# One decoder step in fp32: where the last operand pieces of a gate/up pair stand among the products of the next pair

## The chip, the cores and the metric

The kernel runs on one core of a Trainium2 chip. The metric is device time in microseconds (us) of one execution; lower is better. Engines are named as in the profile: PE (TensorE), DVE (VectorE), ACT (ScalarE), POOL (GpSimd), and SP, whose queue issues the transfers.

## What is computed

One inference step of a two-layer decoder trunk over 1024 prompt tokens and 8 sample tokens, so T = 1032 columns. Each of the two layers ends in a SwiGLU block, and that block is what the change is about:

```python
D_MODEL = 1024
D_FF = -(-8 * D_MODEL // (3 * 256)) * 256   # 2816
...
def swiglu(h, w_gu, w_down):
    g, u = jnp.split(h @ w_gu, 2, axis=-1)
    return (jax.nn.silu(g) * u) @ w_down
...
    for l in range(N_A_LAYERS):
        out, st = short_conv(rmsnorm(x, norm_a[l]), conv_prefix[l], w_in_a[l], conv_w[l], w_out_a[l])
        x = x + out
        x = x + swiglu(rmsnorm(x, norm_ffn[l]), w_gu[l], w_down[l])
...
        x = x + o @ w_o[l]
        li = N_A_LAYERS + l
        x = x + swiglu(rmsnorm(x, norm_ffn[li]), w_gu[li], w_down[li])
```

## The kernel before

Activations lie with features on the 128 partitions and tokens along the free axis. Every fp32 product is made of three matmuls: an operand is split into a high part (ACT copies it to the matmul type) and a low part (DVE subtracts the high part from the operand), and high·high, high·low and low·high are added in PSUM. `split` (lines 147 to 150) does this for weights and activations; `put` (lines 511 to 530) does it for hidden pieces.

The gate and up projections and part of the down projection use a Strassen-like scheme with seven products in place of eight. `gate_up` (line 469) makes 22 units per layer: unit 2m is the gate and unit 2m+1 the up projection of pair m. A unit has the seven products in the order `SEVEN = (1, 5, 6, 3, 7, 2, 4)`. A product is 24 matmuls of 258 columns (two column halves, four blocks of the contraction, three matmuls each). Products 1, 6, 7 and 4 add up in one PSUM tile X, 5 and 3 in Y, 2 in Z. Since product 6 goes on adding to what product 1 left, X must be copied out between them, and so must Y between products 5 and 3:

```python
            if p == 1:
                S.activation(p1[:, s], X, AF.Copy)
            elif p == 5:
                S.activation(p5[:, s], Y, AF.Copy)
```

These are lines 551 to 554 in `gate_step`; they are called **the copy of product 1** (L552) and **the copy of product 5** (L554) below. Product 6 of the gate unit waits for the first and product 3 for the second.

After products 3, 7, 2 and 4 of the up unit the four quarters of silu(gate)·up are complete (`up_step`, lines 570 to 594; the last of them is the multiply of line 593). For pairs 0 to 7 `finish` (line 532) turns them into the seven operands of the seven-product down projection, called pieces 1 to 7: some are quarters, some are differences of quarters. For each piece `put` makes a high part (ACT, L521) and a low part (DVE, L522) in one of four columns of `x` that are used in turn (`ring`, line 478), and SP writes it to DRAM (L524). Pieces 7 and 3 come after product 7; piece 1, a subtraction (L540), piece 5, a subtraction (L542) and piece 6 after product 2; piece 2, a subtraction (L546) and piece 4 after product 4. A slot of the ring is free again when its write has landed: of a pair's seven pieces, piece 6 takes the slot of piece 7, piece 2 that of piece 3, piece 4 that of piece 1.

Weights: `pair_units` (line 416) fetches a unit's weights on SP, POOL forms the four sums that the scheme needs (L446, L448, L450, L452), and ACT and DVE split all seven weight blocks (L149, L150).

The program is recorded in the order of the text, and a scheduler then decides each engine's order. Each engine runs its own list strictly in that order. So the place of an instruction in the text does not say where it stands on its engine.

The words **boundary** and **tail** are used below for the passage from the up unit of pair m to the gate unit of pair m+1, for m from 0 to 7 in each layer (16 in all), and for the pieces that are made there.

Of the kernel before, what the change touches and what calls it, by code (L numbers as in the profile page):

```python
# [13 lines left out]
ALU = mybir.AluOpType  # L14
# [42 lines left out]
def trunk_kernel(ctx, tc, A):  # L57
    nc = tc.nc
    V, S, G, PE, Q = nc.vector, nc.scalar, nc.gpsimd, nc.tensor, nc.sync
# [401 lines left out]
    def col(t, i):  # L461
        return t[:, i * TH : (i + 1) * TH].rearrange("p (s c) -> p s c", s=2)
# [3 lines left out]
    def three_banks():  # L466
        return [pools[-1][0].tile([P, 2, 512], F32, name="mm2") for _ in range(3)]

    def gate_up(layer, us):
# [3 lines left out]
        sg = {  # L473
            q: col(x[:, (3, 7)[i // 2]], i % 2) for i, q in enumerate((11, 12, 21, 22))
        }
# [23 lines left out]
        def group(ps, w, p, s, first):  # L499
            wh, wl = w[p]  # L500
            for k in range(4):
                xh, xl = operand(p, k, s)
                c = slice(k * P, (k + 1) * P)
                for i, (lhs, rhs) in enumerate(((wh, xh), (wh, xl), (wl, xh))):
                    PE.matmul(  # L505
                        ps[:, s, :TS], lhs[:, c], rhs, start=first and k == 0 and i == 0,
                        stop=k == 3 and i == 2, skip_group_check=not first,
                    )
            tick()

        def put(m, src, q=None, p=None):


            nonlocal puts
            k = ring[puts % 4]
            puts += 1
            hi, lo = col(x[:, k], 0), col(x[:, k], 1)
            if src is None:
                G.tensor_tensor(lo, sg[22], sg[12], op=ALU.subtract)  # L519
                src = lo  # L520
            S.activation(hi.bitcast(F32R), src, AF.Copy)  # L521
            V.tensor_tensor(lo.bitcast(F32R), src, hi, op=ALU.subtract)  # L522
            if p is not None:
                Q.dma_start(sd[m, SEVEN.index(p)], x[:, k])  # L524
            else:
                c = slice(TH * (q % 2 == 0), TH * (q % 2 == 0) + TH)
                Q.dma_start(
                    hd[2 * (m - SP) + (q > 20), :, :, c],
                    x[:, k, :].rearrange("p (h c) -> p h c", h=2),
                )  # L530

        def finish(m, q):
            if m >= SP:
                put(m, sg[q], q=q)
            elif q == 22:
                put(m, None, p=7)
                put(m, sg[22], p=3)
            elif q == 11:
                put(m, sg[11], p=1)
                V.tensor_tensor(sg[12], sg[12], sg[11], op=ALU.subtract)  # L540
                put(m, sg[12], p=5)
                V.tensor_tensor(sg[22], sg[22], sg[12], op=ALU.subtract)  # L542
                put(m, sg[22], p=6)
            elif q == 21:
                put(m, sg[21], p=2)
                V.tensor_tensor(sg[21], sg[21], sg[22], op=ALU.subtract)  # L546
                put(m, sg[21], p=4)

        def gate_step(p, banks, s, m):
            X, Y, Z = (b[:, s, :TS] for b in banks)  # L550
# [45 lines left out]
        for n in range(2 * NP):  # L596
            m, step = n // 2, up_step if n % 2 else gate_step
            w = load(n)
            banks = three_banks()

            for subs in ((0,), (1,)) if n == 0 else ((0, 1),):
                for p in (1, 2, 5, 3, 6, 7, 4) if n == 0 else SEVEN:
                    for s in subs:
                        group(banks[BANK[p]], w, p, s, p in (1, 2, 5))
                    sl = slice(subs[0], subs[-1] + 1)
                    if n or p != 3:
                        step(p, banks, sl, m)
                    if n == 0 and p == 6:
                        step(3, banks, sl, m)

# [698 lines left out]
```

## Time and profile before

| | |
|---|---|
| median of three runs | 2283.14 us (2283.0 to 2285.74) |
| the profiled execution | 2284.21 us |
| span of the program in it | 2282.4 us, mean granted TensorE clock 0.976 |
| busy in it | PE 2141.7 us (94%), DVE 1282.7 (56%), POOL 932.5 (41%), ACT 841.3 (37%) |
| chain that ended last | PE 72% of the span, DVE 12%, POOL 5%, ACT 4%, DMA 3% |

The span runs from the first to the last instruction; the profiled execution has 1.8 us outside it. "Busy" of PE means that matmuls were in flight. A time line row gives the start in us from the span's start, the duration in us, the engine, the line and the operands, and in brackets how long the engine had been idle before it and what released it. The chain that ended last is followed back from the last instruction to what released each step. The granted clock of TensorE has two levels, 0.50 (1.2 GHz) and 1.00 (2.4 GHz).

### The profile page before, as it was taken

The page shows a single profiled execution, that of the slowest core. Times are in us where ns is not written, and L with a number is a line of the kernel's source. Part 1 is how long each engine was busy: PE and PEld are TensorE (multiplying, and loading weights), DVE is VectorE, ACT ScalarE, POOL GpSimd, SP SyncE. Part 2 cuts the span into 40 slices and gives each one's busy share as a digit, 9 for nine tenths or more (in the row PEclk, how much of TensorE's full clock was granted, in tenths as well). Part 3 has the DMA queues.
Part 4 walks back from the last instruction along what each step waited for, and adds up shares of the span by engine and source line. Part 5 has one row for each costly group of instructions (what it writes and reads, how often), then busy time and mean ns, then how long its engine had stood idle before and what let it go on. Part 6 is the DMA issues. An engine that isn't in the chain of part 4 may idle for free.

```text
span 2282.4 us, 39301 instructions
## 1 busy us (share of the span) xinstructions
PE 2141.7 (94%) x15754; PEld 2061.2 (90%) x15754; DVE 1282.7 (56%) x2056; ACT 841.3 (37%) x1629; POOL 932.5 (41%) x897
## 2 busy tenths in 40 slices
PE   8999998899999999999999999978999999989997
PEld 7999998798999999999899857767899999989997
DVE  7443447755456444555675476666655655436555
ACT  5110113444444433332322465544444444423322
POOL 5110115434344333553354346674344444336514
PEclk9999998999999999999999999988999999999999
DMA  5111111234324336874054555532433433478532
GB/s 201 39 56 37 56 48 57 65 142 147 121 103 176 118 101 223 308 299 161 19 165 153 143 139 167 161 108 65 167 131 112 167 132 118 133 279 326 213 112 75
DMA packets 138998, 316.24 MB, mean 139 GB/s; under 512 B 14464, under 2 KB 71312, under 8 KB 138656
## 3 DMA queue, kind: packets, MB, share of 16 engines
q1 hardware_dynamic: 138816, 313.74, 40.4%
q8 instruction: 124, 2.03, 0.4%
q14 instruction: 58, 0.48, 0.1%
HBM read 218.26 MB, written 97.54 MB: 138 GB/s over the span
## 4 chain that ended last, share of the span: by engine, by line
PE 72%; DVE 12%; POOL 5%; issue 4%; ACT 4%; DMA 3%; SPq 0%; ACTq 0%; DVEq 0%; POOLq 0%
PE mm L505 27%; PE mm L670 13%; PE mm L139 8%; PE mm L141 8%; PE mm L140 8%; PE po L949 2%; DVE x L522 2%; DVE wl L150 2%; DVE Hl L150 1%; PE sc L915 1%; ACT x L521 1%; POOL acc L164 1%; POOL x L519 1%; DVE x L546 1%; POOL x L586 1%
## 5 line engine op out<-in xcount | busy, mean ns | idle before, releaser
L505 PE MATMUL mm<-Hh,wh 128*128 128x258 f32 x1408 | 407.9, 290 | 36.3 <-ACT inv L554 32.6
L505 PE MATMUL mm<-Hh,wl 128*128 128x258 f32 x1408 | 405.0, 288 | 12.4 <-DVE wl L150 12.4
L505 PE MATMUL mm<-Hl,wh 128*128 128x258 f32 x1408 | 405.4, 288 | 5.6 <-DVE Hl L150 5.6
L139 PE MATMUL mm<-Hh,wh 128*128 128x384 f32 (+2 forms) x1168 | 368.8, 316 | 6.5 <-ACT wh L106 5.7
L140 PE MATMUL mm<-Hl,wh 128*128 128x384 f32 (+2 forms) x1168 | 367.1, 314 | 3.1 <-DVE Hl L228 3.1
L141 PE MATMUL mm<-Hh,wl 128*128 128x384 f32 (+2 forms) x1168 | 365.5, 313 | 3.1 <-POOL wl L107 3.0
L505 PEld LDWEIGHTS mm<-Hh,wh 128*128 128x128 f32 x1408 | 273.4, 194 | 41.3 <-ACT inv L554 36.4
L505 PE MATMUL mm<-exh,wh 128*128 128x258 f32 x1056 | 301.2, 285 | 8.1 <-ACT inv L552 5.9
L150 DVE TENSOR_TENSOR wl<-wraw,wh 128x512 fp32r<-128x512 f32 (+1 forms) x296 | 220.6, 761 | 156.9 <-ACT wh L149 156.5
L505 PE MATMUL mm<-exl,wh 128*128 128x258 f32 x1056 | 298.5, 283 | 1.4 <-DVE exl L150 1.4
L505 PE MATMUL mm<-exh,wl 128*128 128x258 f32 x1056 | 298.5, 283 | 0.0
L505 PEld LDWEIGHTS mm<-Hh,wl 128*128 128x128 f32 x1408 | 273.6, 194 | 12.7 <-DVE wl L150 12.6
L505 PEld LDWEIGHTS mm<-Hl,wh 128*128 128x128 f32 x1408 | 274.1, 195 | 6.0 <-DVE Hl L150 6.0
L149 ACT ACTIVATE wh<-wraw 128x512 fp32r<-128x512 f32 (+1 forms) x296 | 170.3, 601 | 259.0 <-PE mm L505 173.0
L139 PEld LDWEIGHTS mm<-Hh,wh 128*128 128x128 f32 x1168 | 221.5, 190 | 13.3 <-ACT wh L106 5.7
L140 PEld LDWEIGHTS mm<-Hl,wh 128*128 128x128 f32 x1168 | 221.4, 190 | 9.2 <-DVE Hl L228 7.1
L141 PEld LDWEIGHTS mm<-Hh,wl 128*128 128x128 f32 x1168 | 221.2, 189 | 4.9 <-POOL wl L107 3.4
L505 PEld LDWEIGHTS mm<-exh,wh 128*128 128x128 f32 x1056 | 199.7, 189 | 12.8 <-ACT inv L552 9.3
L505 PEld LDWEIGHTS mm<-exl,wh 128*128 128x128 f32 x1056 | 199.7, 189 | 1.8 <-DVE exl L150 1.8
L505 PEld LDWEIGHTS mm<-exh,wl 128*128 128x128 f32 x1056 | 199.5, 189 | 0.1
L164 POOL TENSOR_TENSOR acc<-acc,sq 128x258 f32<-128x258 f32 (+2 forms) x119 | 113.7, 956 | 138.7 <-ACT sq L160 136.3
L446 POOL TENSOR_TENSOR x<-wraw 128x512 f32<-128x512 f32 x40 | 64.7, 1618 | 258.0 <-DMA wraw<-w_gu 258.0
(196 smaller groups left out, 4683.5 us busy)
## 6 DMA issues: line engine op xcount, KB each, us to landing
sd<-x SPq DMA_DIRECT2D x112, 516.0 KB, 3.3
wraw<-w_gu SPq DMA_DIRECT2D x88, 512.0 KB, 3.9
s<-sd SPq DMA_DIRECT2D x48, 516.0 KB, 7.2
Hl<-sd SPq DMA_DIRECT2D x32, 516.0 KB, 8.2
Hh<-sd SPq DMA_DIRECT2D x32, 516.0 KB, 7.6
wraw<-w_down_s SPq DMA_DIRECT2D x32, 512.0 KB, 5.8
wraw<-w_o SPq DMA_DIRECT2D x32, 512.0 KB, 3.8
q<-qd SPq DMA_DIRECT2D x128, 128.0 KB, 2.9
```

Source lines behind the costliest of these rows:

```text
L139: PE.matmul(out, wh[:, c], xh, start=i == 0, stop=False)
L140: PE.matmul(out, wh[:, c], xl, start=False, stop=False)
L141: PE.matmul(out, wl[:, c], xh, start=False, stop=i == n - 1)
L149: S.activation(hi, src, AF.Copy)
L150: eng.tensor_tensor(lo, src, hi.bitcast(F32), op=ALU.subtract)
L164: G.tensor_tensor(acc[:, :w], acc[:, :w], sq[:, :w], op=ALU.add)
L446: G.tensor_tensor(s1, a21, a22, op=ALU.add)
L505: PE.matmul(ps[:, s, :TS], lhs[:, c], rhs, start=first and k == 0 and i == 0, stop=k == 3 and i == 2, skip_group_check=not first,)
L519: G.tensor_tensor(lo, sg[22], sg[12], op=ALU.subtract)
L522: V.tensor_tensor(lo.bitcast(F32R), src, hi, op=ALU.subtract)
L670: PE.matmul(banks[BANK[p]][:, s, :TS], lhs[:, c], rhs, start=first and j == 0 and i == 0, stop=j == 1 and i == 2, skip_group_check=not first,)
L949: PE.matmul(po[r], v[:, 64 * g : 64 * g + 64], p, start=n == 0, stop=n == len(self.pv) - 1,)
```

## The change

In `finish` the piece 5, the second subtraction, pieces 6 and 2, the third subtraction and piece 4 are no longer issued behind products 2 and 4 of the up unit. They are put into a table and issued after products 1, 5, 6 and 3 of the following gate unit. The first subtraction stays where it was. No instruction is added or removed.

```diff
             elif q == 11:
                 put(m, sg[11], p=1)
                 V.tensor_tensor(sg[12], sg[12], sg[11], op=ALU.subtract)
-                put(m, sg[12], p=5)
-                V.tensor_tensor(sg[22], sg[22], sg[12], op=ALU.subtract)
-                put(m, sg[22], p=6)
             elif q == 21:
-                put(m, sg[21], p=2)
-                V.tensor_tensor(sg[21], sg[21], sg[22], op=ALU.subtract)
-                put(m, sg[21], p=4)
+                after_step.update(
+                    {
+                        1: partial(less, m, 5, 12, 22),
+                        5: partial(put, m, sg[22], p=6),
+                        6: partial(put, m, sg[21], p=2),
+                        3: partial(less, m, None, 22, 21, 4),
+                    }
+                )
+
+
+        after_step = {}
+
+        def less(m, p, i, j, p_after=None):
+            if p is not None:
+                put(m, sg[i], p=p)
+            V.tensor_tensor(sg[j], sg[j], sg[i], op=ALU.subtract)
+            if p_after is not None:
+                put(m, sg[j], p=p_after)
...
                     if n or p != 3:
                         step(p, banks, sl, m)
+                    if p in after_step:
+                        after_step.pop(p)()
```

In the changed kernel the lines from 545 on have other numbers: the two moved subtractions are both L557, the multiply of line 593 is L605, and the copies of products 1 and 5 are L564 and L566.

**DVE at a boundary.** Before, from the first subtraction (L540) on. L522 are the low parts of pieces 1, 5, 6, 2 and 4 in this order, L542 and L546 the two later subtractions, L593 the multiply that reads product 4, L150 low parts of weights:

```order
L540 TENSOR_TENSOR x<-x 128x516
L522 TENSOR_TENSOR x<-x 128x516
L542 TENSOR_TENSOR x<-x 128x516
L522 TENSOR_TENSOR x<-x 128x516
L593 TENSOR_TENSOR x<-mm_4389,x 128x516
L522 TENSOR_TENSOR x<-x 128x516
L150 TENSOR_TENSOR wl<-wraw,wh 128x512
L522 TENSOR_TENSOR x<-x 128x516
L546 TENSOR_TENSOR x<-x 128x516
L150 TENSOR_TENSOR wl<-wraw,wh 128x512
L522 TENSOR_TENSOR x<-x 128x516
L150 TENSOR_TENSOR wl<-x,wh 128x512
```

The same stretch in the changed kernel, where L522 are the low parts of pieces 1, 5, 2, and then 6 and 4:

```order
L540 TENSOR_TENSOR x<-x 128x516
L522 TENSOR_TENSOR x<-x 128x516
L605 TENSOR_TENSOR x<-mm_4389,x 128x516
L150 TENSOR_TENSOR wl<-wraw,wh 128x512
L522 TENSOR_TENSOR x<-x 128x516
L557 TENSOR_TENSOR x<-x 128x516
L522 TENSOR_TENSOR x<-x 128x516
L557 TENSOR_TENSOR x<-x 128x516
L522 TENSOR_TENSOR x<-x 128x516 x2
L150 TENSOR_TENSOR wl<-wraw,wh 128x512
L150 TENSOR_TENSOR wl<-x,wh 128x512
```

Between the low part of piece 1 and the last subtraction stood six instructions and now stand five: the low part of piece 6 has gone behind it, and the multiply stands right behind piece 1. The second and third subtraction have only the low part of piece 2 between them. The next unit's weight split stands behind the low part of piece 4, where it stood ahead of it.

**ACT at the same boundary.** Before, from the high part of piece 1 on; L552 and L554 are the copies of products 1 and 5:

```order
L521 ACTIVATE x<-x 128x516
L149 ACTIVATE wh<-wraw 128x512
L521 ACTIVATE x<-x 128x516 x2
L552 ACTIVATE inv<-mm_4626 128x516
L521 ACTIVATE x<-x 128x516
L149 ACTIVATE wh<-wraw 128x512
L521 ACTIVATE x<-x 128x516
L554 ACTIVATE inv<-mm_4627 128x516
L149 ACTIVATE wh<-x 128x512
```

The same in the changed kernel, with L564 and L566 for the two copies:

```order
L521 ACTIVATE x<-x 128x516
L149 ACTIVATE wh<-wraw 128x512
L521 ACTIVATE x<-x 128x516 x2
L564 ACTIVATE inv<-mm_4612 128x516
L521 ACTIVATE x<-x 128x516 x2
L566 ACTIVATE inv<-mm_4613 128x516
L149 ACTIVATE wh<-wraw 128x512
L149 ACTIVATE wh<-x 128x512
```

The pair ahead of the copy of product 1 was pieces 5 and 6 and is now 5 and 2; between the two copies stood piece 2, a weight split and piece 4, and now stand pieces 6 and 4. The order on POOL is unchanged, and that of PE apart from the numbers of its PSUM tiles. On SP the write of piece 2 goes ahead of that of piece 6.

## Rows read from the trace of the kernel before

**Rows 1.** Groups by line, PE: busy, mean ns | idle before and releasers.

```profile
L505 PE MATMUL mm<-Hh,wh 128*128 128x258 f32 x1408 | 407.9, 290 | 36.3 <-ACT inv L554 32.6 <-ACT wh L149 3.0 <-ACT Hh L149 0.6
```

**Rows 2.** Time line of an ordinary boundary, PE's first matmuls of products 6 and 3.

```profile
1778.31 0.39 PE L505 MATMUL mm<-exh,wh 128*128 128x258 f32 x1 [0.23 <-ACT inv L552]
1783.03 0.39 PE L505 MATMUL mm<-Hh,wh 128*128 128x258 f32 x1 [1.59 <-ACT inv L554]
```

**Rows 3.** The same boundary, ACT.

```profile
1777.13 0.64 ACT L521 ACTIVATE x<-x 128x516 fp32r<-128x516 f32 x1 [0.62 <-DVE x L542]
...
1781.86 0.63 ACT L521 ACTIVATE x<-x 128x516 fp32r<-128x516 f32 x1 [2.40 <-DVE x L546]
```

**Rows 4.** The same boundary, DVE, from the low part of piece 1.

```profile
1775.76 0.69 DVE L522 TENSOR_TENSOR x<-x 128x516 fp32r<-128x516 f32 x1
...
1779.38 0.69 DVE L522 TENSOR_TENSOR x<-x 128x516 fp32r<-128x516 f32 x1
1780.11 1.67 DVE L546 TENSOR_TENSOR x<-x 128x516 f32<-128x516 f32 x1
```

**Rows 5.** The same boundary, POOL.

```profile
1778.59 2.63 POOL L446 TENSOR_TENSOR x<-wraw 128x512 f32<-128x512 f32 x1 [7.17 <-DMA wraw<-w_gu]
...
1785.28 1.64 POOL L452 TENSOR_TENSOR x<-wraw 128x512 f32<-128x512 f32 x1
```

**Rows 6.** Chain that ended last: first and last ordinary boundary, then first and last early one.

```profile
650.46 1.68 DVE x L546
...
1908.23 1.68 DVE x L546
...
467.46 1.68 DVE x L522
...
778.88 1.61 DVE x L522
```

**Rows 7.** Time line of an early boundary: DVE, POOL, PE.

```profile
776.45 0.69 DVE L522 TENSOR_TENSOR x<-x 128x516 fp32r<-128x516 f32 x1
...
778.27 0.69 DVE L593 TENSOR_TENSOR x<-mm,x 128x516 f32<-128x516 f32 x1
778.88 1.61 DVE L522 TENSOR_TENSOR x<-x 128x516 fp32r<-128x516 f32 x1
780.41 1.78 DVE L150 TENSOR_TENSOR wl<-wraw,wh 128x512 fp32r<-128x512 f32 x1
...
782.83 0.69 DVE L546 TENSOR_TENSOR x<-x 128x516 f32<-128x516 f32 x1
...
778.65 1.29 POOL L446 TENSOR_TENSOR x<-wraw 128x512 f32<-128x512 f32 x1 [6.53 <-DMA wraw<-w_gu]
...
784.79 0.57 PE L505 MATMUL mm<-Hh,wh 128*128 128x258 f32 x1 [2.65 <-ACT inv L554]
```

**Rows 8.** Time line of the two late boundaries: DVE at 510; DVE, ACT, PE at 1602.

```profile
510.27 0.69 DVE L522 TENSOR_TENSOR x<-x 128x516 fp32r<-128x516 f32 x1
...
516.11 1.66 DVE L546 TENSOR_TENSOR x<-x 128x516 f32<-128x516 f32 x1
...
1602.83 0.69 DVE L522 TENSOR_TENSOR x<-x 128x516 fp32r<-128x516 f32 x1
...
1605.55 0.63 ACT L521 ACTIVATE x<-x 128x516 fp32r<-128x516 f32 x1 [1.96 <-DMA sd<-x]
...
1610.34 0.69 DVE L546 TENSOR_TENSOR x<-x 128x516 f32<-128x516 f32 x1
...
1612.29 0.38 PE L505 MATMUL mm<-Hh,wh 128*128 128x258 f32 x1 [2.44 <-ACT inv L554]
```

**Rows 9.** Windows: us; PE, PEld, DVE, ACT, POOL busy (count); granted clock, DMA share, GB/s.

```profile
474.20:477.60 3.40, 3.40 (x18) 3.40 (x17) 1.11 (x1) 0.18 (x1) 2.17 (x2) 0.50 0.91 306
...
607.30:614.20 6.90, 6.25 (x29) 6.25 (x30) 2.69 (x3) 2.44 (x6) 3.45 (x2) 0.51 0.56 199
...
1783.10:1786.50 3.40, 3.40 (x29) 3.40 (x30) 2.87 (x4) 1.23 (x3) 2.83 (x2) 1.00 0.41 155
```

## The prediction

> **What bounds the kernel now.** I read the groups by line first. In the gate and up units PE loses most of its idle time in one place: of the 36.3 us before the matmuls of high by high, 32.6 end with ACT's L554, the copy of product 5 [rows 1]. There are 16 boundaries in the two layers, so 2.0 us are lost at each. Then the time line of one boundary. Product 6 begins 0.23 us late, behind the copy of product 1, and product 3 at 1783.03, after PE had stood for 1.59 us [rows 2]. Why the copy is late stands one row above it on ACT: its list holds the high part of piece 4 just ahead of the copy, and that one sat idle for 2.40 us for DVE's L546, the last subtraction [rows 3]. Product 5 itself had been ready for long. So the chain runs from DVE's list through L546, ACT's piece 4 and the copy to PE. From the end of L546 (1781.78) to PE's first matmul (1783.03) are 1.25 us.
>
> DVE works without a gap from the low part of piece 1 (1775.76) to L546: five instructions stand between, and the sixth step, to the low part of piece 2, is at 1779.38, so they follow each other by 0.60 us. But L546 follows by 0.73 (to 1780.11), since it overwrites what the one just ahead reads, and it takes 1.67 us, when its like take 0.69 [rows 4]. In that small gap POOL comes in: its L446, whose weights landed at 1778.59, lasted 2.63 us where an unhindered one takes 1.29 [rows 5, 7]. DVE then waits for POOL.
>
> The chain that ended last shows three kinds of boundary. **Ordinary** ones have L546 as the long row: 9, of which [rows 6] shows the first and the last. In 5 **early** ones the long row is L522: POOL's weights land at 778.65, while DVE runs the multiply L593, which takes one operand from PSUM; L446 goes through at once (1.29 us), and two DVE instructions then take 1.61 and 1.78 us. L546 ends at 783.52, 7.07 us after the low part of piece 1 began, against 6.02 at the ordinary one, and PE stands for 2.65 us [rows 4, 7]. In two **late** ones, at 510 and 1602, ACT had waited for a write of the ring in addition (1.96 us, at piece 6); L546 ended 7.50 and 8.20 us after the same mark [rows 8].
>
> Last, the windows. After each early boundary the granted clock fell from 1.00 to 0.50 (1.2 GHz), where PE had stood for 2.65 us [rows 7]: four times for 3.4 us and once for 6.9, of which the first and the long one are shown [rows 9]. After a stand of 1.59 or 2.44 us it stayed at 1.00 [rows 2, 8, 9].
>
> **The change, part by part.** No instruction goes, none comes; POOL's list stays. All four high parts still stand ahead of the copy of product 5 on ACT, whatever the text of the kernel says of "after product 3". What counts is where the last subtraction stands on DVE.
>
> *The last subtraction.* It stands five instructions behind the low part of piece 1, where it stood six behind. Counted from that low part it begins at 5 × 0.60 + 0.73 = 3.7 us, in place of 4.35, and still directly behind the low part of piece 2, so with the same gap. At ordinary boundaries POOL is waiting by then (2.83 us after the mark in [rows 4, 5]). I take the price of L546 for it, 1.67 us: it ends at 5.4 in place of 6.0. That gives 0.6 us at each of 9, 5.5 us. The bounds: 0.69 us, if POOL is not in the way (it ends at 4.4, 1.6 gained), and POOL in twice, each time 1.0 us more, as at early boundaries (6.4, so 0.4 lost). The row nearest in form is L546 itself, the same subtraction behind the same split.
>
> *Early boundaries.* The multiply, through which POOL slipped in, moves from 1.8 us after the mark to 0.6; POOL comes at 2.2 (776.45 to 778.65) and now finds a low part and then a subtraction, both with two operands in SBUF, queued closely. As at ordinary boundaries it should get in only ahead of the last subtraction. L557 then ends at 5.4 in place of 7.07: 1.65 × 5 = 8.3 us.
>
> *Late boundaries.* Ahead of the copy of product 1 now stands piece 2, which takes the slot of piece 3, in place of piece 6 with that of piece 7; the write of piece 3 is issued first of the two, so it should be there sooner. With 5.4 in place of 7.50 and 8.20: 2.1 + 2.8 = 4.9 us.
>
> *The clock.* With PE standing 1.59 − 0.6 = 1.0 us at all boundaries, less than any stand after which it fell, the five drops should go. At half clock a matmul begins every 0.216 us (29 in 6.25 us of PE's time), at full clock every 0.117 (29 in 3.40) [rows 9]. PE worked 4 × 3.4 + 6.25 = 19.9 us in the drops, so they cost 19.9 × (1 − 0.117/0.216) = 9.1 us. The bounds are nothing, if other stands take their place, and all of it.
>
> *The rest.* The copy of product 1 stands behind piece 2 in place of piece 6, and piece 2 waits for the multiply, now where the second subtraction stood: nothing, ±0.1 us. SP's writes of pieces 2 and 6 change places: nothing waits for them. The weight split behind piece 4 comes a little later relative to PE; its cover is treated as a rival.
>
> Sum: 5.5 + 8.3 + 4.9 + 9.1 = 27.8 us. From the profiled 2284.2 this leaves 2256.4; the median of the runs lies 1.1 below that execution, so 2255.
>
> **The rivals.**
>
> *POOL gets in after every DVE instruction.* POOL was ready from 1778.59 and got in at 1780.1, while DVE began two more instructions (at 0.60 us from each other, the last at 1779.38) [rows 4, 5]; so DVE does not give way between queued instructions, and I count on that. But early boundaries show two DVE instructions slowed in a row [rows 7], so it is not sure. POOL, coming at 2.2 to 2.8, would then enter twice, and the last subtraction ends at the 6.4 of above: 0.4 lost at 9, 0.7 gained at 5, 1.1 and 1.8 at the late two. PE's stand of 2.0 us still spares the clock: −3.6 + 3.3 + 2.9 + 9.1 = 11.7 us, 2271. The Trainium skill says the same in "SBUF — State Buffer", section "SBUF: two separate sides": whichever of the two starts first holds the shared port for its whole instruction and the other blocks; by that, POOL's turn would come when the running DVE instruction ends. The trace does not agree at ordinary boundaries: two more DVE instructions began ahead of POOL's [rows 4, 5].
>
> *POOL is not in the way.* If its weights land after 3.7 us, or the gap is too short, L557 takes 0.69 us and PE hardly stands: 1.0 us more at each of 16, 2239. Against it: the landing at 2.2 to 2.8 us in the rows, and the same gap in L546.
>
> *Only the place counts.* Early boundaries stay early and keep their clock drops, since POOL finds another hole: 16 × 0.6 = 9.6 us, 2273.5.
>
> *The change does nothing that can be measured.* The scheduler had already put most pieces among the products; if the tail's end is given by something else than the last subtraction, such as the slot of piece 4, the time stays within 0.2% (4.6 us, about what a measurement of this kernel can tell from no change).
>
> *Slower: the weights of the next unit.* The split L150 stands behind piece 4; POOL's third sum, then L452, wait for it, then a weight split on ACT, and behind that one in ACT's list the copy of product 7, which product 4 needs. L452 ended at 1786.92 [rows 5]; three ACT instructions of 0.6 us (rows of the same kind take 0.63 [rows 3]) end at 1788.8. Product 4 begins after products 3, 7 and 2, each 24 × 0.117 = 2.8 us: at 1791.4 [rows 2, 9]. So 2.6 us are free, and by my sum some 1.1 of them are used (the split 0.5 us later against the mark, PE 0.6 sooner). Beyond 2.6 PE stands at product 4, one for one at 16 boundaries; to eat the gain and add 0.2%, POOL's chain must slip by 2.6 + (28 + 5)/16 = 4.7 us, which gives 2288. Nothing in the rows is near that.
>
> **How the numbers follow.** Forecast 0.56, POOL after every instruction 0.15, not in the way 0.09, only the place 0.09, nothing 0.07, slower 0.04. The forecast alone spans 2249 to 2262 (two of the drops kept and the late boundaries back to ordinary on one side, POOL out of the way at some on the other). The range of 2243 to 2272 takes in the port rival with it (0.71) and the nearer halves of "not in the way" and "only the place" (0.09), and leaves 0.2 out. Faster by over 0.2%: 0.56 + 0.15 + 0.09 + 0.09 = 0.89, less a little for causes that I do not see: 0.88; within 0.2% 0.08; slower 0.04.
>
> **What would show it.** Idle time before high-by-high matmuls that ends with the copy of product 5: 16 × 1.0 to 1.1 us, some 17, in place of 32.6. The last subtraction long (about 1.67 us) at nearly every boundary, with POOL's L446 held ahead of it, and no long L522 ahead of it. Granted clock 1.00 through the gate and up units of both layers behind the first pair. The distance between boundaries the same in both layers, near 42.0 us. The forecast is wrong if L446 goes through at once at some boundaries, if product 3 still starts over 7 us after the low part of piece 1, or if PE now stands at product 6 or 4.

## The result, and the profile after

| | before | after |
|---|---|---|
| median of four runs each | 2284.44 us (2283.0 to 2288.46) | 2253.16 us (2250.63 to 2253.59) |
| the profiled execution | see above | 2253.21 us |
| its span, mean granted TensorE clock | see above | 2251.2 us, 0.981 |

The ratio is 0.9858, 95% interval 0.9841 to 0.9875: faster by 31 us. A second comparison (e11 below) gave 2255.11 us against 2282.71, ratio 0.9884 (0.9866 to 0.9901): faster by 27.6 us. The prediction was 2255.0 us, and 27.8 us of gain.

First the groups by line of the changed kernel, PE, against [rows 1]:

```profile
L505 PE MATMUL mm<-Hh,wh 128*128 128x258 f32 x1408 | 403.8, 287 | 19.3 <-ACT inv L566 15.7 <-ACT wh L149 3.0 <-ACT Hh L149 0.5
```

The idle time that ends with the copy of product 5 fell from 32.6 to 15.7 us, 0.98 a boundary. The two smaller waits stand as they were.

Then the time line of the changed kernel at the boundary that was the last early one before [rows 7]: DVE from the low part of piece 1, then POOL, ACT, PE. The start of that low part is called **the mark** from here on.

```profile
759.23 0.69 DVE L522 TENSOR_TENSOR x<-x 128x516 fp32r<-128x516 f32 x1
759.84 0.69 DVE L605 TENSOR_TENSOR x<-mm,x 128x516 f32<-128x516 f32 x1
760.44 0.68 DVE L150 TENSOR_TENSOR wl<-wraw,wh 128x512 fp32r<-128x512 f32 x1
761.04 0.69 DVE L522 TENSOR_TENSOR x<-x 128x516 fp32r<-128x516 f32 x1
761.64 0.69 DVE L557 TENSOR_TENSOR x<-x 128x516 f32<-128x516 f32 x1
762.25 0.69 DVE L522 TENSOR_TENSOR x<-x 128x516 fp32r<-128x516 f32 x1
762.98 1.67 DVE L557 TENSOR_TENSOR x<-x 128x516 f32<-128x516 f32 x1
...
761.37 2.71 POOL L446 TENSOR_TENSOR x<-wraw 128x512 f32<-128x512 f32 x1 [6.47 <-DMA wraw<-w_gu]
...
764.72 0.63 ACT L521 ACTIVATE x<-x 128x516 fp32r<-128x516 f32 x1 [1.67 <-DVE x L557]
765.26 0.58 ACT L566 ACTIVATE inv<-mm 128x516 f32<-128x516 f32 x1
...
765.90 0.39 PE L505 MATMUL mm<-Hh,wh 128*128 128x258 f32 x1 [0.99 <-ACT inv L566]
```

POOL's weights landed 2.14 us after the mark, as early as at this boundary before (2.20), but this time L446 did not go through: its row lasts 2.71 us where an unhindered one lasts 1.29, so it was held for some 1.4 us, until the gap ahead of the last subtraction (762.25 + 0.60 would be 762.85; it began at 762.98). That one took 1.67 us and ended 5.42 us after the mark, in place of 7.07, and product 3 began at 6.67 in place of 8.34. Fifteen of the 16 boundaries read so, in both layers, to 0.02 us. The exception is the first of layer 1 (mark 1579.12): POOL came at 4.03 us, the last subtraction was short (0.69), but piece 4's high part then waited for a write of the ring, and product 3 began at 6.50.

Last the windows of the changed kernel at the places that answer to three of the kernel before, against [rows 9]:

```profile
471.90:475.30 3.40, 3.40 (x28) 3.40 (x29) 2.38 (x5) 1.46 (x4) 1.60 (x1) 1.00 0.66 257
765.90:769.30 3.40, 3.40 (x28) 3.40 (x29) 2.38 (x5) 1.48 (x3) 1.60 (x1) 1.00 0.65 263
1753.70:1757.10 3.40, 3.40 (x28) 3.40 (x29) 2.38 (x5) 1.46 (x4) 1.60 (x1) 1.00 0.59 232
```

No boundary is followed by a lower clock any more.

Where the 31.0 us between the two profiled executions went, by PE's same matmuls in both: 18.9 had been gained at the last boundary of layer 0 (784.79 before, 765.90 after), and 1.5 more just behind it, where the last of the five drops had been. The boundaries of layer 1 gave 7.8 (23.7 us ahead at their start, 31.5 at their end). Together 28.2. The other 2.8 came in the main between the layers (20.4 us ahead behind layer 0, 23.7 at the start of layer 1), in steps at drops of the clock that lay elsewhere in the two executions.

### The profile page after: what moved, and what is told of

It is laid out like the page before. It is cut to its first block, busy times and chain, and to the rows that moved or that the text cites. A ratio compares the mean times of both kernels' runs of the same rounds, so it can differ in the third digit from the quotient of the medians.

```text
span 2251.2 us, 39285 instructions
## 1 busy us (share of the span) xinstructions
PE 2132.6 (95%) x15754; PEld 2053.5 (91%) x15754; DVE 1278.5 (57%) x2056; ACT 842.4 (37%) x1629; POOL 927.4 (41%) x897
## 4 chain that ended last, share of the span: by engine, by line
PE 72%; DVE 11%; POOL 5%; ACT 4%; issue 4%; DMA 3%; SPq 0%; ACTq 0%; DVEq 0%; POOLq 0%
PE mm L505 27%; PE mm L684 13%; PE mm L139 9%; PE mm L141 8%; PE mm L140 8%; PE po L963 2%; DVE x L557 2%; DVE wl L150 2%; DVE Hl L150 1%; PE sc L929 1%; DVE x L522 1%; ACT x L521 1%; POOL x L519 1%; POOL x L598 1%; POOL x L597 1%
## 5 line engine op out<-in xcount | busy, mean ns | idle before, releaser
L505 PE MATMUL mm<-Hh,wh 128*128 128x258 f32 x1408 | 403.8, 287 | 19.3 <-ACT inv L566 15.7
L150 DVE TENSOR_TENSOR wl<-wraw,wh 128x512 fp32r<-128x512 f32 (+1 forms) x296 | 211.5, 731 | 158.6 <-ACT wh L149 156.3
L522 DVE TENSOR_TENSOR x<-x 128x516 fp32r<-128x516 f32 x136 | 120.7, 897 | 95.9 <-ACT x L521 92.9
L446 POOL TENSOR_TENSOR x<-wraw 128x512 f32<-128x512 f32 x40 | 66.7, 1667 | 256.8 <-DMA wraw<-w_gu 256.8
```

The lines of the kernel that those rows point to most:

```text
L150: eng.tensor_tensor(lo, src, hi.bitcast(F32), op=ALU.subtract)
L446: G.tensor_tensor(s1, a21, a22, op=ALU.add)
L505: PE.matmul(ps[:, s, :TS], lhs[:, c], rhs, start=first and k == 0 and i == 0, stop=k == 3 and i == 2, skip_group_check=not first,)
```

## The experiments

The theory to test: PE's stand at product 3 is made by a chain, the last subtraction, ACT's piece 4, the copy of product 5; POOL lengthens the last subtraction because it can enter only in a gap of DVE, or while the multiply runs; the clock follows the stand. Rivals: POOL enters behind any DVE instruction; only the place of the last subtraction counts; the chain doesn't go over ACT's list; the drops have another cause. Medians, with the kernel before on the same chip:

| run | us | before | ratio (95%) |
|---|---|---|---|
| e1 weight split between | 2242.17 | 2280.05 | 0.983 (0.9816 to 0.9845) |
| e2 piece 4 behind copy 5 | 2238.28 | 2280.05 | 0.9814 (0.98 to 0.9829) |
| e3 second half alone | 2239.44 | 2280.05 | 0.9828 (0.9808 to 0.9849) |
| e4 first half alone | 2291.14 | 2280.05 | 1.0048 (1.0031 to 1.0065) |
| e5 two copies first | 2245.13 | 2282.59 | 0.9827 (0.9798 to 0.9855) |
| e6 before's order, two copies | 2236.02 | 2282.59 | 0.978 (0.9748 to 0.9813) |
| e7 e1 and e5 together | 2241.65 | 2282.59 | 0.9809 (0.9783 to 0.9835) |
| e8 longer stand | 2301.26 | 2282.59 | 1.0074 (1.0048 to 1.01) |
| e9 piece 4 behind copy 6 | 2227.36 | 2282.71 | 0.9759 (0.9738 to 0.978) |
| e10 the same, before's order | 2225.13 | 2282.71 | 0.9757 (0.9736 to 0.9778) |
| e11 the change again | 2255.11 | 2282.71 | 0.9884 (0.9866 to 0.9901) |

### e1: no gap ahead of the last subtraction

```diff
-                split(wh, wl, src)
+                S.activation(wh, src, AF.Copy)
+                low = partial(V.tensor_tensor, wl, src, wh.bitcast(F32), op=ALU.subtract)
+                if len(out) == 6 and hold:
+                    held.append(low)
+                else:
+                    low()
...
+        def rest(m):
+            less(m, 5, 12, 22)
+            put(m, sg[21], p=2, shift=1)
+            tc.keep_in_program_order(held.pop()())
+            last = V.tensor_tensor(sg[21], sg[21], sg[22], op=ALU.subtract)
+            tc.keep_in_program_order(last)
+            put(m, sg[22], p=6, shift=-1, behind=last)
+            put(m, sg[21], p=4)
```

`rest` is called after product 1; `keep_in_program_order` adds an edge of issue order to the instruction recorded before on the same engine, `shift` keeps each piece in its slot of the ring, and one more edge keeps the copy of product 5 behind piece 4 on ACT, as in the change.

> All instructions of the changed kernel, ACT's list as it was; on DVE one weight split (the subtraction for the last quarter of the gate unit's weights, in the changed kernel third behind the mark, ahead of the low part of piece 5) now stands between the low part of piece 2 and the last subtraction. So the last subtraction still stands five instructions behind the mark, but what it overwrites has been read by then, and the 0.73 us step ahead of it (3.02 to 3.75 in the changed kernel) should become the common one of 0.60. Theory (POOL enters in a gap of DVE, not behind each instruction): POOL's first weight sum, asked for 2.1 to 3.5 us after the mark, finds no gap until the last subtraction is over; that one begins at 3.63 and takes 0.69 in place of 1.66 us, ends at 4.3, product 3 begins at 5.6 in place of 6.67, 1.1 us less at each of 16 boundaries: 2253.2 - 17.6 = 2235.6 us. Rival 1 (the port goes to POOL when the running DVE instruction ends, or only the place on DVE counts): some instruction between 2.1 and 4 us is still the long one, the last subtraction ends at 5.3 or later, and the time stays at 2251 to 2254. Rival 2 (the sum that POOL gets later now makes the next unit's weights late): product 3 early, but a new wait behind weights, time 2240 to 2253.

The time line of this run, first boundary, DVE then POOL. L563 is the weight split, L564 the last subtraction, L530 the low parts, L453 POOL's first sum.

```profile
464.54 0.69 DVE L530 TENSOR_TENSOR x<-x 128x516 fp32r<-128x516 f32 x1
...
466.96 0.68 DVE L530 TENSOR_TENSOR x<-x 128x516 fp32r<-128x516 f32 x1
467.56 0.68 DVE L563 TENSOR_TENSOR wl<-wraw,wh 128x512 fp32r<-128x512 f32 x1
468.17 0.68 DVE L564 TENSOR_TENSOR x<-x 128x516 f32<-128x516 f32 x1
468.77 2.40 DVE L530 TENSOR_TENSOR x<-x 128x516 fp32r<-128x516 f32 x2
...
466.73 3.89 POOL L453 TENSOR_TENSOR x<-wraw 128x512 f32<-128x512 f32 x1 [6.52 <-DMA wraw<-w_gu]
```

The last subtraction begins 3.63 us after the mark and takes 0.68; POOL, ready at 2.19, waits until 470.62 − 1.29 = 469.3, while DVE begins four more instructions. The last subtraction is as short at all 16 boundaries; at 15 of them POOL asked before it began, between 2.17 and 3.50 us after the mark. So neither the place nor the instruction makes the subtraction long, but the gap of 0.12 us ahead of it: 0.12 us of place and 1 us of POOL are told apart here. The rival in which POOL gets in behind any DVE instruction falls. The Trainium skill, "SBUF — State Buffer", section "SBUF: two separate sides", says that whichever of the two starts first has the shared port for the whole instruction; the trace agrees in that POOL, once it had entered, kept a DVE instruction waiting (the two low parts behind the last subtraction take 2.40 us). It disagrees if "starts" is read as POOL's turn after the running instruction: POOL had none in 2.6 us of DVE instructions back to back.

Idle time with the copy of product 5 fell from 15.7 to 2.2 us. What is left are five boundaries at which piece 4's high part waits for a write of the ring (product 3 stands 0.20 to 0.83 us). The time fell by less than the 17.6 us expected: it is 2242.2 us, where the change's two ratios, 0.9858 and 0.9884, would give 2247.7 and 2253.6 on this chip. That lies in the range of rival 2 (2240 to 2253), but no new wait for weights is behind it. In the profiled pair the boundaries gained 14.7 us (1.1 each at ten, 0.6 to 1.0 at five, nothing at the first of layer 1), and 5 were lost outside them (see e11).

### e2: piece 4 behind the copy of product 5

```diff
-            S.activation(hi.bitcast(F32R), src, AF.Copy)
+            ahead = {4: 5}.get(p)
+            with tc.issue_after(copy[ahead].ins) if ahead else nullcontext():
+                S.activation(hi.bitcast(F32R), src, AF.Copy)
```

> The changed kernel, DVE's list the same up to the last subtraction; on ACT the high part of piece 4 is held behind the copy of product 5 by an order of issue alone. Theory (product 3 is late only because the copy of product 5 stands behind the high part of piece 4, which waits for the last subtraction): the copy now waits for nothing on DVE, product 3 follows product 6 at once (5.4 us after the mark in place of 6.67), though the last subtraction is as long as before (1.66 us, to 5.4). 16 x 1.14 us: 2253.2 - 18 = 2235 us. Rival (the stand only moves: the copy of product 6 or the next weight splits, now behind piece 4, are late instead, or another wait of product 3 ends there): product 3 early, product 7 or 4 late, 2245 to 2253.

The groups by line, PE, of this run, and its DVE, ACT and PE at one boundary, mark 749.57 (L560 the last subtraction, L569 the copy of product 5):

```profile
L505 PE MATMUL mm<-Hh,wh 128*128 128x258 f32 x1408 | 402.2, 286 | 4.0 <-ACT wh L149 3.0 <-ACT Hh L149 0.6 <-ACT x L583 0.2
```

```profile
753.31 1.68 DVE L560 TENSOR_TENSOR x<-x 128x516 f32<-128x516 f32 x1
...
753.81 0.58 ACT L569 ACTIVATE inv<-mm 128x516 f32<-128x516 f32 x1
...
755.11 0.28 PE L505 MATMUL mm<-Hh,wh 128*128 128x258 f32 x1
```

The copy of product 5 no longer appears among the releasers, while DVE's last subtraction is as long as in the change (1.67 us, to 5.42). Each boundary is 1.25 us shorter (1.1 at the first of layer 1), 20 us in all. The chain over ACT's list is shown: with one edge of order, which puts piece 4 behind the copy, the same late subtraction costs nothing at product 3. The time is 2238.3 us where 2235 was expected, and the rival's 2245 and above did not come. Of the 20 us the medians show 9 to 15 (2247.7 or 2253.6 for the change on this chip, as under e1). In the profiled pair 14.0 are left: outside the boundaries this execution lost 6. It spent 103 us at half clock in all, the change's first profile 86 (see e11).

### e3 and e4: the halves of the change

e3 gives pieces 5 and 6 at once, as before, and only the rest late; e4, the second diff, gives only piece 6 late.

```diff
             elif q == 11:
...
+                put(m, sg[12], p=5)
+                V.tensor_tensor(sg[22], sg[22], sg[12], op=ALU.subtract)
+                put(m, sg[22], p=6)
             elif q == 21:
-                        1: partial(less, m, 5, 12, 22),
-                        5: partial(put, m, sg[22], p=6),
                         6: partial(put, m, sg[21], p=2),
                         3: partial(less, m, None, 22, 21, 4),
```

```diff
             elif q == 11:
...
+                put(m, sg[12], p=5)
+                V.tensor_tensor(sg[22], sg[22], sg[12], op=ALU.subtract)
             elif q == 21:
+                put(m, sg[21], p=2)
+                V.tensor_tensor(sg[21], sg[21], sg[22], op=ALU.subtract)
+                put(m, sg[21], p=4)
-                        1: partial(less, m, 5, 12, 22),
                         5: partial(put, m, sg[22], p=6),
-                        6: partial(put, m, sg[21], p=2),
-                        3: partial(less, m, None, 22, 21, 4),
```

> One half of the change: pieces 5 and 6 and the subtraction between them are given at once as before, only piece 2, the last subtraction and piece 4 among the products of the next gate unit. DVE's list is that of the kernel before (multiply fourth, last subtraction sixth behind the mark, same self-made gap), but on ACT the copy of product 5 comes ahead of the high part of piece 4. Theory: DVE's rows look as before (last subtraction to 6.0 us behind the mark, at some boundaries 7.07 with two long instructions), and yet PE does not stand at product 3: 2235 us, as in the run with piece 4 held behind the copy. Rival (the end of DVE's tail sets the end, by whatever path): no better than before at 2284, or at best the 2253 of the whole change.

> The other half: only piece 6 is given after product 5, the rest at once. On ACT piece 4 stays ahead of the copy of product 5. On DVE the last subtraction stands five instructions behind the mark as in the whole change, but the multiply stays third (1.8 us behind the mark, when POOL's sum is asked for at 2.1 to 3.5) and the low part of piece 2, which needs its result through ACT, comes right ahead of the last subtraction. Theory: a gap of some 0.15 us ahead of the low part of piece 2 lets POOL in there, which ends the tail at 5.7 (product 3 at 6.9), and where POOL comes during the multiply it goes through at once and two long instructions follow (product 3 at 7.6 or later): early boundaries stay, with clock drops. The copy of product 1 is earlier, so PE stands at product 3 longer than in the change, not at product 6. 2260 to 2270 us. Rival (only the place of the last subtraction counts): 2253, as the whole change. Rival (the half does nothing): 2284.

e3's groups by line, PE, and its DVE and ACT at the first boundary (L558 the last subtraction, L567 the copy of product 5):

```profile
L505 PE MATMUL mm<-Hh,wh 128*128 128x258 f32 x1408 | 402.0, 286 | 4.0 <-ACT wh L149 3.0 <-ACT Hh L149 0.5 <-ACT inv L567 0.3
```

```profile
469.10 1.67 DVE L558 TENSOR_TENSOR x<-x 128x516 f32<-128x516 f32 x1
...
468.36 0.58 ACT L567 ACTIVATE inv<-mm 128x516 f32<-128x516 f32 x1
470.85 0.64 ACT L521 ACTIVATE x<-x 128x516 fp32r<-128x516 f32 x1 [1.92 <-DVE x L558]
```

DVE's tail is that of before (4.35 + 1.67 = 6.02 us after the mark [rows 4], and long pairs at 4 boundaries where POOL came during the multiply), yet PE does not stand at product 3: the scheduler happened to place the copy ahead of piece 4. At those 4 boundaries product 7 begins 0.3 to 0.5 us late instead, and at the second boundary (mark 505.51) product 6 stands 0.97 us. By the medians half of the change does more than the whole of it: 2239.4 us against 2247.7 or 2253.6.

e4 came out slower than the kernel before, where 2260 to 2270 us was expected. Its DVE (L607 the multiply, L545 the last subtraction), POOL and PE at one boundary, mark 1778.12:

```profile
1779.94 0.69 DVE L607 TENSOR_TENSOR x<-mm,x 128x516 f32<-128x516 f32 x1
1780.54 0.68 DVE L150 TENSOR_TENSOR wl<-wraw,wh 128x512 fp32r<-128x512 f32 x1
1781.37 1.55 DVE L522 TENSOR_TENSOR x<-x 128x516 fp32r<-128x516 f32 x1 [0.15 <-ACT x L521]
1782.95 1.65 DVE L545 TENSOR_TENSOR x<-x 128x516 f32<-128x516 f32 x1
...
1780.95 1.42 POOL L446 TENSOR_TENSOR x<-wraw 128x512 f32<-128x512 f32 x1 [7.17 <-DMA wraw<-w_gu]
1782.44 1.60 POOL L448 TENSOR_TENSOR wraw<-wraw 128x512 f32<-128x512 f32 x1
...
1785.81 0.39 PE L505 MATMUL mm<-Hh,wh 128*128 128x258 f32 x1 [2.48 <-ACT inv L568]
```

The expected gap of 0.15 us is there, and POOL enters in it. What was not counted: POOL's second sum, L448, is ready right behind the first and takes the next gap, the one ahead of the last subtraction, so that two DVE instructions are long, and the tail ends at 6.48, not 5.7. PE stands for 2.48 us, and the clock falls behind 15 of the 16 boundaries. The miss is one of size: per boundary the price lacked one POOL instruction and a drop of the clock. The two long rows of [rows 7] read the same way: two sums of POOL, not one.

### e5 to e7: the next thing in ACT's list

```diff
-            ahead = {4: 5}.get(p)
+            ahead = {4: 5, 2: 1}.get(p)
```

This is e5 against e2. e6 has `{4: 5, 6: 1}` and gives piece 5 and the second subtraction at once, as e3, and piece 6 after product 1; DVE's list is then that of before, but for one weight split that stands ahead of the low part of piece 6 in place of behind it. e7 is e1's order on DVE with e5's table.

> The run with piece 4 behind the copy of product 5, and in addition the high part of piece 2 held behind the copy of product 1 on ACT. ACT sits idle from 0.76 to 1.38 us behind the mark there, and the copy (0.58 us) fits. On DVE the low part of piece 6 comes to stand between the low part of piece 2 and the last subtraction, with a gap ahead of it, since its high part ends on ACT only at 3.8. Theory: POOL's sum gets in at that gap, so the low part of piece 6 is the long instruction and the last subtraction ends at 6.2 or later, later than in the changed kernel (5.4); and yet PE stands neither at product 6 (0.40 us before) nor at product 3: 16 x 0.4 = 6.4 us less than with piece 4 alone, 2238.3 - 6.4 = 2232 us on the chip of that run. Rival (the end of the tail still counts, through the weights or through piece 4): 2238 or above.

> Pieces 5, the second subtraction and the multiply stand on DVE as in the kernel before; on ACT the copy of product 1 is ahead of pieces 6 and 2, the copy of product 5 ahead of piece 4. DVE's tail is then at least as long as before. Theory (the order on ACT alone decides): as the run with two copies first, 2232 us, within 3 us. Rival (the changed order on DVE gives a part of its own): 2240 or above.

> The order on DVE of the run with the weight split between (no gap, the last subtraction over at 4.3 us) together with both copies first on ACT. If the place of the last subtraction and POOL's collision cost only through the copy of product 5, this gives nothing beyond the run with two copies first: the same time within 3 us, though the tail ends some 2 us earlier on DVE. Rival (a shorter tail or a later POOL also moves something else): over 4 us apart, in either direction.

e5 was 13 us slower than the 2232 expected (on another chip; against the kernel before on its own, some 11). Its DVE, ACT and PE at one boundary, mark 1744.34 (L560 the last subtraction, L571 the copy of product 6):

```profile
1748.20 1.55 DVE L524 TENSOR_TENSOR x<-x 128x516 fp32r<-128x516 f32 x1 [0.15 <-ACT x L523]
1749.68 1.77 DVE L560 TENSOR_TENSOR x<-x 128x516 f32<-128x516 f32 x1
...
1748.59 0.58 ACT L569 ACTIVATE inv<-mm 128x516 f32<-128x516 f32 x1
1751.53 0.64 ACT L523 ACTIVATE x<-x 128x516 fp32r<-128x516 f32 x1 [2.36 <-issue]
1752.07 0.61 ACT L149 ACTIVATE wh<-x 128x512 fp32r<-128x512 f32 x1
1752.59 0.58 ACT L571 ACTIVATE u<-mm 128x516 f32<-128x516 f32 x1
...
1753.23 0.39 PE L505 MATMUL mm<-exh,wh 128*128 128x258 f32 x1 [0.81 <-ACT u L571]
```

Products 6 and 3 are on time, but product 7 now waits, by the same mechanism one copy later: the copy of product 6 stands behind piece 4, whose subtraction ends 7.1 us after the mark, since POOL's two sums have both found a gap, as in e4. (The profile names no releaser for piece 4's high part, "issue"; it begins 0.08 us behind the end of L560.) The rival of e5 holds, at 15 of the 16 boundaries. In e6 the ordinary boundaries have no stand at all (40.28 us from mark to mark), and at the 5 with POOL in the multiply product 7 begins 0.92 to 1.03 us later than there (0.76 to 0.86 of it is idle time of PE). In e7 it begins 0.55 us late at 13 boundaries and on time at 3. POOL's first sum (L453), held in e1's gapless order, now delays the high part of a weight split (L445) that is ahead of the copy of product 6 (L585) on ACT:

```profile
1743.55 4.44 POOL L453 TENSOR_TENSOR x<-wraw 128x512 f32<-128x512 f32 x1 [7.18 <-DMA wraw<-w_gu]
...
1748.02 0.63 ACT L445 ACTIVATE wh<-x 128x512 fp32r<-128x512 f32 x1 [2.28 <-POOL x L453]
1748.56 0.58 ACT L585 ACTIVATE u<-mm 128x516 f32<-128x516 f32 x1
```

So the three are up to 9 us apart, and what decides is again which copy ACT holds back. The two other expectations missed with e5's: e6 is 9 us faster than e5, not the same within 3, and below its rival's 2240; e7 is 3.5 us faster, between its theory and its rival.

### e8: a longer stand

```diff
+            for _ in range(1 + (1, 2)[layer] * (p == 4)):
+                copy["hi"] = S.activation(hi.bitcast(F32R), src, AF.Copy)
```

The copy of product 5 is held behind the last of them by an edge of issue order.

> The changed kernel with the high part of piece 4 written once more in layer 0 and twice more in layer 1 (the same values), ahead of the copy of product 5, and in its gaps the order on ACT lets one weight split (0.62 us) pass. PE's stand at product 3 becomes 1.15 + 1.25 = 2.4 us in layer 0 and 1.15 + 1.9 = 3.05 in layer 1. Theory (a granted clock of 0.50 follows a long stand, whatever the layer): in layer 1 a drop behind all or nearly all boundaries, which before and in the change had none; in layer 0, near the 2.46 and 2.60 us after which it stayed at 1.00 before and the 2.52 after which it fell in the run with the first half alone, some or none. Time, against the 2253 of the change: 8 x 1.25 + 8 x 1.9 = 25 us of standing and 8 x 1.6 = 13 of clock, 2291, up to 2304 with drops in layer 0 too. Rival (the drops have another cause than the stand): 25 us of standing alone, 2278.

PE's matmuls of product 3 in one boundary of layer 0 and two of layer 1, then the windows that follow them:

```profile
472.71 0.39 PE L505 MATMUL mm<-Hh,wh 128*128 128x258 f32 x1 [2.02 <-ACT inv L572]
...
1652.11 0.58 PE L505 MATMUL mm<-Hh,wh 128*128 128x258 f32 x1 [3.06 <-ACT inv L572]
...
1697.47 0.39 PE L505 MATMUL mm<-Hh,wh 128*128 128x258 f32 x1 [3.07 <-ACT inv L572]
```

```profile
474.00:477.40 3.40, 3.40 (x18) 3.40 (x17) 1.07 (x2) 0.30 (x1) 2.06 (x2) 0.50 0.94 324
1651.60:1655.00 3.40, 2.89 (x13) 2.89 (x14) 1.86 (x2) 0.95 (x2) 2.91 (x2) 0.50 0.99 340
1697.50:1700.90 3.40, 3.40 (x28) 3.40 (x29) 1.50 (x2) 0.71 (x2) 2.39 (x2) 1.00 1.00 350
```

The drops are back, 7 behind the 8 boundaries of layer 0 and 6 behind the 8 of layer 1, where there were none before: the longer stand brings them, though not each time, and the layer is not their cause. The time, 2301.3 us, is in the range of the theory (2291 to 2304) and far from the rival's 2278, though the stand in layer 0 was 2.02 us and not 2.4. Behind two boundaries of layer 1 the clock stayed at 1.00, which prices a drop within one run: from mark to mark 44.10 us without one, 45.4 to 45.6 with one of 3.4 us, 46.6 to 46.75 with one of 6.8. So 1.3 to 1.5 and 2.5 to 2.65 us, where the prediction had 1.6 and 2.9.

### e9 to e11: the version that beats both

```diff
-            ahead = {4: 5, 2: 1}.get(p)
+            ahead = {4: 6, 2: 1}.get(p)
```

This is e9 against e5; e10 is e6 with `{4: 6, 6: 1}`, and e11 the changed kernel as it is.

> As the run with two copies first, whose PE stood 0.97 us at product 7 because the copy of product 6 waited on ACT behind the high part of piece 4 (last subtraction over at 7.1 us behind the mark). Here the high part of piece 4 is held behind that copy too. Theory (each stand at a boundary is a copy that ACT holds back behind a piece): no stand at product 6, 3 or 7, though DVE's tail is as long; the distance between boundaries falls from 41.36 us to the 40.28 that the run with the copies in the order of before showed at boundaries without a stand: 16 x 1.08 = 17 us off 2245, 2228. Rival (piece 4, now later, holds back the copy of product 7 or the weights): a stand at product 2 or 4, 2235 or above.

> The order on DVE of the kernel before, with the high part of piece 4 held behind the copy of product 6: the run with the copies in the order of before had 0.92 to 1.03 us of stand at product 7 at 5 of 16 boundaries, where POOL came during the multiply. Theory: those go too, 5 us off 2236, 2231, and so the same within 4 us as the run with the changed order on DVE and piece 4 behind the copy of product 6: what stands where on DVE then costs nothing. Rival: over 6 us between the two.

> The changed kernel once more, beside the last two on the same chip. Theory: 0.986 of the kernel before, the same 42.0 us between boundaries; on the matter of clock drops outside the boundaries, if they are laid out by chance from run to run their places between 870 and 1550 us differ from the first profile (883.8, 914.5, 1119.3, 1259.3, 1433.3, 1511.8, 1542.6), if they are fixed by the kernel they fall in the same places within 4 us.

The groups by line of e10, PE, products 3 and 7 among them, and two instructions of its DVE at the first boundary, mark 464.10, of which POOL lengthens the first and not the second (L150 behind the multiply, L561 the last subtraction):

```profile
L505 PE MATMUL mm<-Hh,wh 128*128 128x258 f32 x1408 | 401.9, 286 | 3.8 <-ACT wh L149 3.0 <-ACT Hh L149 0.5 <-ACT inv L570 0.3
...
L505 PE MATMUL mm<-exh,wh 128*128 128x258 f32 x1056 | 299.6, 284 | 1.8 <-ACT u L577 1.4 <-ACT u L572 0.3
```

```profile
466.52 1.78 DVE L150 TENSOR_TENSOR wl<-wraw,wh 128x512 fp32r<-128x512 f32 x1
...
470.64 0.70 DVE L561 TENSOR_TENSOR x<-x 128x516 f32<-128x516 f32 x1
```

No stand is left at products 6, 3 and 7, at 40.3 us from mark to mark in both. e9 came out at 2227.4 (expected 2228), e10 at 2225.1 (expected 2231), the same within the theory's 4 us, although e10's tail on DVE ends as late as 7.24 us after the mark. Once ACT's list is right, neither of these two orders on DVE costs anything that shows; and e10 has very nearly before's, with the high parts of pieces 6, 2 and 4 moved on ACT. It is 30 us faster than the change on the same chip, and 57.6 faster than before.

e11's boundaries are as long as those of the first profile to 0.05 us. Of the seven drops between the layers that its expectation lists, four are in their places within 4 us, and three begin 7 to 10 us earlier (1112.3 for 1119.3 is one). Two more, at 1399.0 and 1463.8, the first profile did not have. So neither of the two answers that were expected holds by itself: most drops come back near the same place, and some come and go from one execution to the next. Set matmul against matmul with the first profile, this execution of the same kernel lost 4.6 us between 1270 and 1520 us, where its additional drops lie; e1 lost 8.8 and e2 5.9 in the same stretch, where they too have more drops than the first profile. That the drops also make the difference between the two comparisons of the change is not shown. What starts them was not tried.

## Why the prediction was right

*What bounds the kernel.* The chain DVE, last subtraction, ACT's piece 4, copy of product 5, PE is shown by e2 and e3: cut on ACT, PE's stand goes, with DVE as late as ever. From the end of the last subtraction to product 3 are 6.67 − 5.42 = 1.25 us after, as before.

*The last subtraction.* Forecast: begins at 3.7 us after the mark, takes 1.67, ends at 5.4. Measured: 3.75, 1.67, 5.42. Ordinary boundaries give 7.28 − 6.67 = 0.61 us, forecast 0.6. That POOL enters in the gap and not behind any instruction was taken from a few rows of one boundary; e1 shows it by closing the gap.

*Early boundaries.* Forecast 1.65 each, measured 8.28 to 8.39 less 6.67, 1.61 to 1.72. That the multiply lets POOL through was right too: in the five kernels where it stands 1.82 us after the mark (before, e3, e4, e6, e10), all 23 sums that asked between 2.06 and 2.35 us went through at once.

*Late boundaries.* Forecast 2.1 and 2.8; measured 8.75 − 6.67 = 2.1 and 9.46 − 6.50 = 3.0. The second came by another way than forecast: POOL was late there and not in the way, and a write of the ring held piece 4 instead.

*The clock.* Forecast 9.1 us for five drops, and all five went. In layer 0, where they lay, the sum was 2 × 0.6 + 5 × 1.65 + 2.1 + 9.1 = 20.7 us; measured 18.9 + 1.5 = 20.4. The drops alone can be read in the kernel before: its early boundaries are 45.13 to 45.25 us from mark to mark with a drop of 3.4 us, 46.49 with the one of 6.8, where the change has 42.0; less the 1.61 to 1.72 by which product 3 was later, that is 1.5 and 2.8 us, 8.8 for the five. The reason was right as far as a longer stand brings drops (e8), the threshold behind it was not: "less than any stand after which it fell" is true of the 1.0 us that came, but e8 had drops after 2.02 us and none after 3.07, and e4 one after 1.80. Had the stand come out at 2 us, as in the first rival, the 9.1 us counted there as spared would not have been safe.

*The weights of the next unit* did not become a bound: no wait at product 4 appeared in the change. In e7, where POOL's first sum took 4.2 to 5.2 us in place of 1.4 to 2.7, a weight split did hold PE, at product 7; the mechanism exists, but not in the change.

*The sum.* 27.8 us forecast, 28.2 on the boundaries and behind them in the profiled pair, 31.3 and 27.6 between the medians of the two comparisons. What the prediction did not see is the larger gain one list further: it noted that all four high parts still stand ahead of the copy of product 5 on ACT, and took that as given. Two edges of order there (e9) are worth another 28 us, and with before's order on DVE (e10) 30.

## What to carry to other kernels

When an engine waits for a copy that is short and whose input is long ready, look at what stands ahead of it in its own engine's list before shortening the work that the thing ahead waits for: one edge of order there (e2) took away a stand that re-ordering the list of another engine had only shortened. Expect the wait to turn up at the next copy in the same list, and fix the whole row. And when one engine holds up another in the gaps of its list, as POOL does DVE here, count every instruction that it has ready, since one gap after the other is taken (e4: two long instructions in place of one).

## What was not expected of the hardware

POOL's chance ends sharply. With the multiply (one operand in PSUM) running from 1.82 to 2.51 us after the mark, a sum that asked at 2.35 got through at once, and one that asked at 2.36 waited for 1.8 us, to the next gap. Both are in e10's POOL rows, at the marks 464.10 and 1805.60:

```profile
466.45 1.30 POOL L446 TENSOR_TENSOR x<-wraw 128x512 f32<-128x512 f32 x1 [6.69 <-DMA wraw<-w_gu]
```

```profile
1807.95 3.11 POOL L446 TENSOR_TENSOR x<-wraw 128x512 f32<-128x512 f32 x1 [6.69 <-DMA wraw<-w_gu]
```

The next DVE instruction begins at 2.42, so in these runs a sum had to be there 0.07 us ahead of it, while the multiply still ran; one 0.06 us ahead was held. And the clock does not follow the length of a stand alone: at 1.00 behind 3.07 us (e8), 2.44 [rows 8], at 0.50 behind 2.02 (e8) and 1.80 (e4).
